# Gates of 32 more tokens placed by indirect transfers into a second table, with an order of norms at the seams of the feed-forward blocks

## The chip, the cores and the metric

The kernel runs on one core of one Trainium2 chip, alone. The metric is the device time of one execution in microseconds; runs are compared by their medians. On this core TensorE (PE) does the matrix products, VectorE (DVE) and ScalarE (ACT) the elementwise work, POOL (GpSimd) a little elementwise work and the transfers that it issues itself, and SP only issues transfers.

## What is computed

Two blocks run one after the other on 256 tokens of width 1024, in float32. The first has a gated recurrent branch and an attention branch, and after them a mixture over 16384 experts, which is the part that matters here. The second has four SwiGLU feed-forward blocks, a convolution block and a blockwise attention, each with a norm before and after it. Cut to the expert layer and the feed-forward:

```python
t1, i1 = lax.top_k(s1, 16); t2, i2 = lax.top_k(s2, 16)      # per token and head, of 128 keys each
cand = t1[..., :, None] + t2[..., None, :]                  # 16 x 16 candidates
ts, sel = lax.top_k(cand, 16)
idx = (i1 * 128 + i2) at sel
g = softmax(ts)
act = gelu(einsum('chkd,cd->chk', u[idx], xt))
out = einsum('chk,chkd->cd', g * act, v[idx])               # 8 heads x 16 experts per token

f = (silu(h @ w_gate) * (h @ w_up)) @ w_down                # feed-forward, 256 x 1024 -> 2816 -> 1024
x = x + 0.5 * rms_norm(f, g_post)
```

## The kernel before

The expert layer gathers nothing. It multiplies all 256 tokens with all 16384 rows of `peer_u`, takes the gelu, multiplies every value by the token's gate for that expert (zero for most), and multiplies the result with all of `peer_v`. The tile `C` (128 x 128 x 256) holds it: partition j and plane a stand for the expert with the two indices a and j, and the last axis is the token. Every float32 matrix operand is split into a high and a low part (`units`, L115, for weights: ScalarE writes the high half of a `ws` tile at L147, VectorE the low half at L150), and a product is three matmuls (`mm3`, L195 to L199).

The gates reach `C` in two ways. Tokens 0 to 127 are routed one head at a time (`routing_by_head`, L868). Each head gives 16 experts and 16 gates for each of 128 tokens, and POOL adds them to a table `gd` in DRAM (cleared before) with 16 indirect transfers, each of one element from each of 128 partitions (L914). Tokens 128 to 255 are routed together (`routing`, L792). Their gates are placed by `scatter` (L920), four tokens a call: VectorE and ScalarE build one-hot tiles `oh`, TensorE multiplies them (L934, four matmuls of 128 x 128), and the product goes into `C` as the factor of the gelu that is there or will come. The generator `work` (L944) hands this out in pieces between the loads of the gating stage: `peer_u` comes in 64 loads, and after each of them `advance` emits pieces up to a budget. There are 32 calls of `scatter`.

The table is cleared early: while the weights of the first projections are loaded, `clear` (L327), called at each load, adds one transfer of zeros to SP's queue, 16 of 512 KB in all.

In the expert-value stage `peer_v` comes in 64 loads, two for each group of four planes. For each of the 32 groups `gates_of` (L1030) issues from POOL a load of that group's gates of tokens 0 to 127 into one of two `x` tiles, two groups ahead; `gated_c` (L1035) multiplies four planes of `C` by it on VectorE, and `coef` (L1044) splits the group into the high and low parts that TensorE takes as the stationary side (`vgo`, L1022).

A feed-forward block (`ffn`, L1112) walks over 11 slices of its width. At its end the two halves of the tokens are taken apart: for token half 0 the post norm (`post`, L1079) and the next block's norm `nx(0)` (L1108, with `norm_only`, L246, which writes `xn` in two halves on VectorE at L253) are emitted, then the last gate and up products of half 1 (`GU`, L1119, whose result `hh` VectorE writes at L1130), then its transposes (`TR`, L1138), down products and, between them, the transposes of half 0's `xn` (`run(p0)`). I call this place a seam; there are three with a following norm that is transposed there (after blocks 0, 1 and 2).

The order on each engine is made by the Tile scheduler from the order of the program and the dependences; `after` (L162) adds an order between two instructions without a semaphore. The few lines to keep in mind:

```python
for k in range(16):                                           # routing_by_head, 16 transfers a head
    i = nc.gpsimd.indirect_dma_start(gflat, ...slot[:, h, k:k + 1]..., gate[:, h, k:k + 1], None, compute_op=ALU.add)
for k in range(32):                                           # work
    scatter(T - 4 - 4 * k, work.bound)
for t in range(2):                                            # vgo per unit of peer_v
    mm3(acc[t][half], (c[:, 0, ai % 4, ts_], c[:, 1, ai % 4, ts_]), (pair[0][:, s], pair[1][:, s]), ...)
```

## Time and profile before

| | |
|---|---|
| median of 3 runs | 2111.91 us (2111.25 to 2112.9) |
| the profiled execution, time | 2111.61 us |
| its span | 2109.8 us |
| PE busy | 2058.6 us (98%) |
| DVE busy | 1414.7 us (67%) |
| ACT busy | 1156.8 us (55%) |
| POOL busy | 347.7 us (16%) |
| DMA | 386.66 MB, mean 183 GB/s |

The span is that of the instructions in the trace; the 1.8 us beside it lie outside. Busy time is the sum of the durations of an engine's instructions, overlaps counted once. A matmul's end is modelled and successive matmuls overlap, so what one costs is read from start to start. The stages, in us from the span's start: projections, recurrent branch and attention to about 286, gating with `peer_u` to about 736, expert values with `peer_v` to about 1087, and then the second block.

### The profile page before, as it was taken

Reading aid. Unit: us, or ns where it says so; the run is one execution under the profiler, and the core shown is the slowest. Engines: PE = TensorE matmul, PEld = TensorE weight load, DVE = VectorE, ACT = ScalarE, POOL = GpSimd, SP = SyncE. Lnnn points to the kernel's source line nnn. Section 1 sums busy time; section 2 is a strip of 40 time slices with the busy share of each in tenths; the row PEclk is TensorE's granted clock in tenths of the full one; section 3 lists DMA queues with packets and bytes.
Section 4 is the critical chain, followed back from the end, with each engine's and each line's share of the span. In section 5 each row is a group of like instructions: output and inputs, shape, how many; then the busy total and the mean of one; then the engine's idle time right before and its main releaser. Section 6 shows DMA issues by size and latency. Waiting matters only on the chain.

```text
span 2109.8 us, 31786 instructions
## 1 busy us (share of the span) xinstructions
PE 2058.6 (98%) x12526; PEld 1825.8 (87%) x12526; DVE 1414.7 (67%) x2523; ACT 1156.8 (55%) x1872; POOL 347.7 (16%) x262
## 2 busy tenths in 40 slices
PE   7999999999999999999999999989999999999998
PEld 7899989999999988888878888878887888887886
DVE  6675668898877566566566665966666665756564
ACT  5885444555776444444455555565554554655553
POOL 2000007777750000000000001920000000000000
PEclk9999999999999999999999999999999999999999
DMA  8742546676654566665666554226555554744551
GB/s 269 256 141 92 178 165 164 194 184 181 179 141 146 196 213 210 215 214 206 218 246 246 182 197 142 100 72 240 196 180 173 206 182 157 263 167 180 180 196 64
DMA packets 91797, 386.66 MB, mean 183 GB/s; under 512 B 25968, under 2 KB 28144, under 8 KB 59904
## 3 DMA queue, kind: packets, MB, share of 16 engines
q1 hardware_dynamic: 70656, 376.17, 51.5%
q0 software_dynamic: 20992, 8.46, 3.1%
q8 instruction: 98, 1.61, 0.3%
q14 instruction: 51, 0.42, 0.1%
HBM read 372.87 MB, written 10.55 MB: 182 GB/s over the span
## 4 chain that ended last, share of the span: by engine, by line
PE 86%; DVE 6%; ACT 3%; DMA 2%; issue 2%; POOL 1%; SPq 0%; POOLq 0%; DVEq 0%; ACTq 0%
PE pa L197 19%; PE pa L199 19%; PE pa L198 19%; PE pt L184 6%; PE pm L184 6%; PE pt L186 3%; PE pm L186 3%; PE pm L197 2%; PE pm L199 2%; PE pm L198 2%; DVE pa L1310 2%; DVE ws L150 1%; PE pm L934 1%; ACT ws L147 1%; PE pt L234 1%
## 5 line engine op out<-in xcount | busy, mean ns | idle before, releaser
L150 DVE TENSOR_TENSOR ws<-raw,ws 128x1024 fp32r<-128x1024 f32 (+1 forms) x661 | 807.4, 1228 | 486.8 <-ACT ws L147 484.7
L147 ACT ACTIVATE ws<-raw 128x1024 fp32r<-128x1024 f32 (+1 forms) x665 | 697.4, 1056 | 577.5 <-PE pa L199 367.3
L197 PE MATMUL pa<-xT,ws 128*128 128x256 f32 x1280 | 363.6, 285 | 0.7 <-ACT g L1596 0.5
L198 PE MATMUL pa<-xT,ws 128*128 128x256 f32 x1280 | 361.4, 283 | 0.0
L199 PE MATMUL pa<-xT,ws 128*128 128x256 f32 x1280 | 361.1, 282 | 0.0
L197 PEld LDWEIGHTS pa<-xT,ws 128*128 128x128 f32 x1280 | 242.1, 189 | 1.8 <-ACT g L1596 1.0
L198 PEld LDWEIGHTS pa<-xT,ws 128*128 128x128 f32 x1280 | 242.2, 189 | 0.1
L199 PEld LDWEIGHTS pa<-xT,ws 128*128 128x128 f32 x1280 | 242.0, 189 | 0.1
L914 POOL DMA_INDIRECT gd<-gate,slot x128 | 225.4, 1761 | 99.0 <-DVE slot L909 39.1
L220 POOL TENSOR_TENSOR rr<-rs,mhalf 128x1 f32<-128x1 f32 (+1 forms) x36 | 32.3, 897 | 1203.1 <-DVE rs L218 1199.0
L198 PE MATMUL pa<-ws,ch 128*128 128x512 f32 x512 | 201.9, 395 | 0.0
L199 PE MATMUL pa<-ws,ch 128*128 128x512 f32 x512 | 201.8, 395 | 0.0
L197 PE MATMUL pa<-ws,ch 128*128 128x512 f32 x512 | 201.2, 395 | 0.0
L184 PE MATMUL pt<-xT,ws 128*128 128x512 f32 x512 | 190.6, 394 | 0.0
L184 PE MATMUL pm<-xT,ws 128*128 128x512 f32 x512 | 190.4, 394 | 0.0
L197 PE MATMUL pa<-ws,hT 128*128 128x512 f32 x352 | 139.9, 397 | 0.6 <-ACT hT L202 0.5
L199 PE MATMUL pa<-ws,hT 128*128 128x512 f32 x352 | 139.1, 395 | 0.3 <-DVE hT L203 0.3
L198 PE MATMUL pa<-ws,hT 128*128 128x512 f32 x352 | 139.0, 395 | 0.0
L186 PE MATMUL pm<-xT,ws 128*128 128x256 f32 x448 | 125.6, 280 | 0.0
L186 PE MATMUL pt<-xT,ws 128*128 128x256 f32 x448 | 125.6, 280 | 0.0
L197 PEld LDWEIGHTS pa<-ws,ch 128*128 128x128 f32 x512 | 96.5, 188 | 22.6
L198 PEld LDWEIGHTS pa<-ws,ch 128*128 128x128 f32 x512 | 96.5, 188 | 22.6 <-DVE ws L150 0.3
(454 smaller groups left out, 3868.0 us busy)
## 6 DMA issues: line engine op xcount, KB each, us to landing
raw<-in_ffn_dram SPq DMA_DIRECT2D x132, 1024.0 KB, 4.9
raw<-in_peer_u_dram SPq DMA_DIRECT2D x64, 1024.0 KB, 5.0
raw<-in_peer_v_dram SPq DMA_DIRECT2D x64, 1024.0 KB, 4.8
raw<-in_win_dram SPq DMA_DIRECT2D x16, 1024.0 KB, 4.9
gain<-in_gains_dram SPq DMA_DIRECT2D x17, 512.0 KB, 5.2
gd<-zero SPq DMA_DIRECT2D x16, 512.0 KB, 7.9
raw<-in_wpq_dram SPq DMA_DIRECT2D x8, 1024.0 KB, 5.1
x<-gd POOLq DMA_DIRECT2D x32, 256.0 KB, 4.7
```

The source lines that it names most:

```text
L147: i = nc.scalar.activation(hi, r, AF.Copy)
L150: self.last = (eng or nc.vector).tensor_tensor(out=lo, in0=r, in1=hi.bitcast(F32), op=ALU.subtract)
L184: nc.tensor.matmul(o, wp[0], v, start=first, stop=last)
L186: nc.tensor.matmul(o[:, 0:256], wp[1], v[:, 0:256], start=False, stop=False)
L197: nc.tensor.matmul(o, wh, xh, start=first, stop=False)
L198: nc.tensor.matmul(o, wh, xl, start=False, stop=False)
L199: nc.tensor.matmul(o, wl, xh, start=False, stop=last)
L220: nc.gpsimd.tensor_tensor(out=r2[:rows], in0=r[:rows], in1=mhalf[:rows], op=ALU.pow)
L234: nc.tensor.transpose(p[:, j * rows:(j + 1) * rows], src[:rows, (b + j) * 128:(b + j + 1) * 128], ident[:rows, :rows])
L914: i = nc.gpsimd.indirect_dma_start(gflat, bass.IndirectOffsetOnAxis(ap=slot[:, h, k:k + 1], axis=0), gate[:, h, k:k + 1], None, compute_op ...
L934: nc.tensor.matmul(p[:, k * 128:(k + 1) * 128], oh[:, k, 0:128], oh[:, k, 128:256], start=True, stop=True)
L1310: nc.vector.scalar_tensor_tensor(out=o, in0=u, scalar=w, in1=acc, op0=ALU.mult, op1=ALU.add)
```

## The change

Four things are done.

1. Tokens 128 to 159 leave `scatter`: it is called 24 times instead of 32. Their gates go into a second table `gd4` in DRAM by 32 indirect transfers (`by_quarters`): the 8 heads of a token are taken as four quarters of two heads, the indices and gates of 32 tokens x 128 are brought into a tile of 4 x 32 partitions by eight small transfers from POOL, and each of the 32 transfers places one element for each of 128 (quarter, token) pairs. In the table each quarter has its own 32 columns of a plane's 128.
2. `gates_of` loads from both tables, so POOL issues two loads of 256 KB a group instead of one. `gated_c` gets three POOL operations more, which add the four quarters together (64 columns, then 32, of four planes) and multiply `C` of tokens 128 to 159 by the sum. The second table is cleared by eight more transfers of zeros, of 1 MB each.
3. Each indirect transfer waits for the completion of all 16 of the group before its own (`wait_for`), and the first two groups' loads of the tables wait for all transfers of the last two groups.
4. At the seams of `ffn` the norm `nx(0)` is emitted behind `GU((1,), f)`, and its two `xn` instructions are ordered behind `GU.last`, the last `hh`.

```diff
+    gd4 = dp.tile([128, 128 * 128], F32, name="gd4")
...
+    def wait_for(i, js):
+        for j in js:
+            tc.add_manual_dep(i.ins, j.ins.name, mybir.DependencyInfo(mybir.DependencyClass.Sync, mybir.DependencyReason.DATA), reason="same elements")
...
-            nc.vector.scalar_tensor_tensor(out=xn[:rows, s], in0=src[:, s], scalar=r[:rows], in1=g[:rows, s], op0=ALU.mult, op1=ALU.mult)
+            i = nc.vector.scalar_tensor_tensor(out=xn[:rows, s], in0=src[:, s], scalar=r[:rows], in1=g[:rows, s], op0=ALU.mult, op1=ALU.mult)
+            if behind is not None:
+                after(i, behind)
...
-            if 0 <= i < ZN:
+            if 0 <= i < 3 * ZN // 2:
                 w = 128 * 128 // ZN
+                dst, i, w = (gd, i, w) if i < ZN else (gd4, i - ZN, 2 * w)
...
+                wait_for(i, placed[-16 - k:-k or None])
+                placed.append(i)
...
+        def by_quarters():
+            V = nc.vector
+            s0 = sl[:, 0].rearrange("p h k -> p (h k)")
+            V.tensor_scalar(s0, sli[:, 1], 128.0 * 128, tokf, ALU.mult, ALU.add)
+            V.scalar_tensor_tensor(out=s0, in0=sli[:, 0], scalar=128.0, in1=s0, op0=ALU.mult, op1=ALU.add)
+            V.tensor_tensor(out=sli[:, 0], in0=s0, in1=quarter, op=ALU.add)
+            for q in range(4):
+                s = slice(32 * q, 32 * q + 32)
+                nc.gpsimd.dma_start(slq[s], sli[0:32, 0, s])
+                nc.gpsimd.dma_start(gaq[s], sl[0:32, 2].rearrange("p h k -> p (h k)")[:, s])
+            for j in range(32):
+                i = nc.gpsimd.indirect_dma_start(qflat, bass.IndirectOffsetOnAxis(ap=slq[:, j:j + 1], axis=0), gaq[:, j:j + 1], None,
+                                                 compute_op=ALU.add)
+                wait_for(i, placed[-16 - j % 16:-(j % 16) or None])
+                placed.append(i)
...
-            for k in range(32):
+            by_quarters()
+            yield 8, 0.8
+            for k in range(24):
...
-            v = x_tile()[:, 0:512].rearrange("p (a t) -> p a t", a=4)
-            nc.gpsimd.dma_start(v, gd[:, 512 * g:512 * (g + 1)].rearrange("p (a t) -> p a t", a=4))
+            v = x_tile().rearrange("p (k a t) -> p k a t", k=2, a=4)
+            for i, table in enumerate((gd, gd4)):
+                i = nc.gpsimd.dma_start(v[:, i], table[:, 512 * g:512 * (g + 1)].rearrange("p (a t) -> p a t", a=4))
+                if g < 2:
+                    wait_for(i, placed[-32:])
...
-            G(nc.vector.tensor_tensor(out=c, in0=c, in1=gl.pop(0), op=ALU.mult))
+            v = gl.pop(0)
+            G(nc.vector.tensor_tensor(out=c, in0=c, in1=v[:, 0], op=ALU.mult))
+            w, c = v[:, 1], C[:, 4 * g:4 * g + 4, 128:160]
+            nc.gpsimd.tensor_tensor(out=w[:, :, 0:64], in0=w[:, :, 0:64], in1=w[:, :, 64:128], op=ALU.add)
+            nc.gpsimd.tensor_tensor(out=w[:, :, 0:32], in0=w[:, :, 0:32], in1=w[:, :, 32:64], op=ALU.add)
+            nc.gpsimd.tensor_tensor(out=c, in0=c, in1=w[:, :, 0:32], op=ALU.mult)
...
-            p0 = nx(0)
             GU((1,), f)
+            p0 = nx(0, GU.last)
```

The order that the scheduler makes of it, at the places of which the prediction speaks. First VectorE at the seam after the first feed-forward block, before the change (`hh` is the product of gate and up half, `xn` the normed tokens, `ws` a weight's low half, `hT` the low half of the transposed `hh`):

```order
L150 TENSOR_TENSOR ws<-raw,ws 128x1024
L253 SCALAR_TENSOR_TENSOR xn<-x,rr,gain 128x512 x2
L1130 TENSOR_TENSOR hh<-pm,sg 128x256
L150 TENSOR_TENSOR ws<-raw,ws 128x1024
L203 TENSOR_TENSOR hT_12333<-pt,hT_12332 128x2x128
```

And with the change:

```order
L152 TENSOR_TENSOR ws<-raw,ws 128x1024
L1177 TENSOR_TENSOR hh<-pm,sg 128x256
L259 SCALAR_TENSOR_TENSOR xn<-x,rr,gain 128x512 x2
L209 TENSOR_TENSOR hT_12397<-pt,hT_12396 128x2x128
L152 TENSOR_TENSOR ws<-raw,ws 128x1024
```

`hh` now stands ahead of `xn`, right behind the same `ws`, and `hT` ahead of the next `ws`. At the third seam one `ws` stays between `xn` and `hT`; elsewhere the three are alike. TensorE's order there is all but the same in both, and what is to be noted in it is that the transposes of `xn` come right behind those of `hh`:

```order
L240 MATMUL pt<-ident,hh 128x128 x2
L240 MATMUL pt<-ident,xn 128x128 x4
L203 MATMUL pa<-ws,hT_12396 128x512
L204 MATMUL pa<-ws,hT_12396 128x512
L203 MATMUL pa<-ws,hT_12396 128x512
L205 MATMUL pa<-ws,hT_12397 128x512
```

Last POOL's queue with the change, from the heads' transfers to the steady state of the expert-value stage (`gd_67` is the second table):

```order
L924 DMA gd<-gate,slot 2097152x1 x64
L969 DMA gaq<-sl 32x32 x4
L924 DMA gd<-gate,slot 2097152x1 x32
L968 DMA slq<-sli 32x32 x4
L924 DMA gd<-gate,slot 2097152x1 x32
L971 DMA gd_67<-gaq,slq 2097152x1 x32
L1072 DMA x<-gd 128x512
L1072 DMA x<-gd_67 128x512
...
L1082 TENSOR_TENSOR x<-x 128x4x64
L1083 TENSOR_TENSOR x<-x 128x4x32
L1084 TENSOR_TENSOR C<-C,x 128x4x32
```

Before, the heads' 128 transfers are followed directly by the 32 gate loads, with nothing between them. From the fifth group on, the last five of these rows repeat for each group, and the first of the three operations waits for the load just ahead of it.

## Rows read from the trace of the kernel before

**Rows 1.** The page, part 4: the chain that ended last, by engine.

```profile
PE 86%; DVE 6%; ACT 3%; DMA 2%; issue 2%; POOL 1%; SPq 0%; POOLq 0%; DVEq 0%; ACTq 0%
```

**Rows 2.** Two stages: PE, PEld, DVE, ACT, POOL busy us, clock, DMA share, GB/s.

```profile
555.00:690.00 135.00, 135.00 (x1156) 135.00 (x1155) 101.97 (x185) 93.69 (x231) 47.87 (x30) 1.00 0.52 152
...
735.00:1075.00 340.00, 340.00 (x1476) 276.05 (x1476) 203.26 (x186) 160.62 (x157) 15.31 (x28) 1.00 0.61 211
```

**Rows 3.** Who TensorE waited for, whole span: us in total, times, longest.

```profile
PE pt L234 <- DVE hh L1130: 5.7, 3, 2.0
```

**Rows 4.** TensorE's timeline round one pair of scatter steps: start, us, instruction.

```profile
671.32 0.28 PE L199 MATMUL pa<-xT,ws 128*128 128x256 f32 x1
671.44 1.95 PE L934 MATMUL pm<-x 128*128 128x128 f32 x16
673.14 0.36 PE L197 MATMUL pa<-xT,ws 128*128 128x256 f32 x1
673.35 0.27 PE L198 MATMUL pa<-xT,ws 128*128 128x256 f32 x1
```

**Rows 5.** VectorE's timeline at the end of the first feed-forward block.

```profile
1282.34 1.22 DVE L150 TENSOR_TENSOR ws<-raw,ws 128x1024 fp32r<-128x1024 f32 x1
1284.00 1.41 DVE L253 SCALAR_TENSOR_TENSOR xn<-x,rr,gain 128x512 f32<-128x512 f32 x2 [0.44 <-POOL rr L220]
1285.33 0.42 DVE L1130 TENSOR_TENSOR hh<-pm,sg 128x256 f32<-128x256 f32 x1
```

**Rows 6.** TensorE's timeline at the same place.

```profile
1285.80 0.44 PE L234 MATMUL pt<-ident,hh 128*128 128x128 f32 x2 [1.98 <-DVE hh L1130]
1286.07 0.60 PE L234 MATMUL pt<-ident,xn 128*128 128x128 f32 x4
1286.71 0.55 PE L197 MATMUL pa<-ws,hT 128*128 128x512 f32 x1
```

**Rows 7.** The stretches behind the first two seams, columns as in rows 2.

```profile
1285.00:1300.00 15.00, 13.64 (x87) 12.18 (x88) 11.12 (x18) 8.98 (x15) 1.48 (x2) 0.89 0.60 209
...
1605.00:1625.00 20.00, 18.89 (x90) 15.18 (x91) 14.94 (x24) 9.89 (x19) 1.95 (x2) 1.00 0.68 239
```

**Rows 8.** Transfers issued from 24 to 45 us: KB each, median us to landing.

```profile
raw<-in_win_dram SPq DMA_DIRECT2D x3, 1024.0 KB, 7.3
```

**Rows 9.** SP's timeline: the third weight load of the projection stage.

```profile
110.97 0.33 SPq L131 DMA_DIRECT2D raw<-in_win_dram  x1
```

**Rows 10.** ScalarE's timeline: the first use of that load.

```profile
117.90 1.05 ACT L147 ACTIVATE ws<-raw 128x1024 fp32r<-128x1024 f32 x1
```

**Rows 11.** POOL's timeline: second head's first transfer, the last transfer, two gate loads.

```profile
357.29 1.54 POOL L914 DMA_INDIRECT gd<-gate,slot  x1 [4.00 <-DVE wk L800]
...
612.73 1.54 POOL L914 DMA_INDIRECT gd<-gate,slot  x1 [0.30 <-issue]
...
888.97 0.55 POOL L1032 DMA_DIRECT2D x<-gd  x1 [10.62 <-DVE C L1037]
...
900.13 0.55 POOL L1032 DMA_DIRECT2D x<-gd  x1 [10.61 <-DVE C L1037]
```

**Rows 12.** POOL by line and form: busy us, mean ns of one, idle before.

```profile
L914 POOL DMA_INDIRECT gd<-gate,slot x128 | 225.4, 1761 | 99.0 <-DVE slot L909 39.1 <-issue 37.1 <-DVE ws L150 6.8
...
L150 POOL TENSOR_TENSOR ws<-raw,ws 128x1024 fp32r<-128x1024 f32 x4 | 9.4, 2374 | 5.5 <-ACT ws L147 5.5
...
L1329 POOL TENSOR_TENSOR pw<-pw 128x256 f32<-128x256 f32 x1 | 1.6, 1588 | 0.1
```

**Rows 13.** VectorE's timeline where the expert-value stage begins.

```profile
731.55 1.29 DVE L1037 TENSOR_TENSOR C<-C,x 128x512 f32<-128x512 f32 x2
```

**Rows 14.** Transfers issued from 735 to 850 us, columns as in rows 8.

```profile
x<-gd POOLq DMA_DIRECT2D x10, 256.0 KB, 4.7
```

**Rows 15.** VectorE's timeline in the convolution.

```profile
1317.08 4.05 DVE L150 TENSOR_TENSOR ws<-raw,ws 128x1024 fp32r<-128x1024 f32 x2
```

**Rows 16.** POOL's timeline at the same time.

```profile
1317.24 2.81 POOL L1326 TENSOR_TENSOR pw<-ud,pv 128x1024 f32<-128x1024 f32 x1 [16.77 <-DVE ud L1346]
```

More of the change, by code (lines that the diff above doesn't have):

```diff
@@ L244, in norm_T, with norm_only @@
         norm_only(src, g, wk, rows, r, (hi, lo, off))()
-    def norm_only(src, g, wk, rows, r, dst):
+    def norm_only(src, g, wk, rows, r, dst, behind=None):
         hi, lo, off = dst
@@ L328, in clear @@
             i -= ZFROM
-            if 0 <= i < ZN:
+            if 0 <= i < 3 * ZN // 2:
                 w = 128 * 128 // ZN
-                nc.sync.dma_start(gd[:, i * w:(i + 1) * w].rearrange("p (r w) -> p r w", w=512),
+                dst, i, w = (gd, i, w) if i < ZN else (gd4, i - ZN, 2 * w)
+                nc.sync.dma_start(dst[:, i * w:(i + 1) * w].rearrange("p (r w) -> p r w", w=512),
                                   zero.unsqueeze(1).to_broadcast([128, w // 512, 512]))
@@ L755, in _body @@
         st.aside = None
-        assert st.calls >= ZFROM + ZN
+        assert st.calls >= ZFROM + 3 * ZN // 2
         dump("h1", X[0])
@@ L863, in _body @@
         posu1 = cp.tile([128, 16], U32, name="posu1")
+        placed = []
         gflat = gd.rearrange("p (e o) -> (p e) o", o=1)
@@ L939, in scatter @@
                 nc.scalar.activation(C[:, bound:128, t0:t0 + 4], v[:, bound:128, :], AF.Copy)
+        quarter = cp.tile([128, 128], I32, name="quarter")
+        nc.gpsimd.iota(quarter, [[32, 4], [0, 32]], base=0, channel_multiplier=0)
+        slq = cp.tile([128, 32], I32, name="slq")
+        gaq = cp.tile([128, 32], F32, name="gaq")
+        qflat = gd4.rearrange("p (e o) -> (p e) o", o=1)
+        def by_quarters():
[13 more added lines that the diff above has]
+                placed.append(i)
+                tc.declare_no_dep(i.ins, group="quads%d" % (j // 16), reason="other elements")
+                tc.add_to_no_dep_group("quads%d" % (j // 16), i.ins)
         class Scattered:
@@ L1015, in _body @@
             advance(WQBUD * 8 + BUD * (n + 1) if n < 62 else 1e9)
-        assert Scattered.done == 128
+        assert Scattered.done == 96
         dump("idT", idT)
@@ L1106, in __init__, with __call__ @@
                 self.xT = [joined(alloc) for _, alloc in items]
-            def __call__(self, t):
+            def __call__(self, t, behind=None):
                 r = rstd([X[t]], D, bp)
-                return [norm_only(X[t], g, bp, 128, r, (x[0], x[1], t * 128)) for g, x in zip(self.g, self.xT)]
+                return [norm_only(X[t], g, bp, 128, r, (x[0], x[1], t * 128), behind) for g, x in zip(self.g, self.xT)]
         def ffn(i, xT, nxt, pend):
@@ L1129, in GU @@
                     nc.scalar.activation(sg, p[t][:, 0:256], AF.Silu)
-                    nc.vector.tensor_tensor(out=h, in0=p[t][:, 256:512], in1=sg, op=ALU.mult)
+                    GU.last = nc.vector.tensor_tensor(out=h, in0=p[t][:, 256:512], in1=sg, op=ALU.mult)
                     hh[t, f] = h
@@ L1634, in _body, with __call__ @@
             xT = None
-            def __call__(self, t):
+            def __call__(self, t, behind=None):
                 for half in range(2):
```

## The prediction

> **What bounds the kernel now.** I read the chain of waits first: 86% of it is TensorE, and no other engine has over 6% [rows 1]. So time is won by taking instructions from TensorE or by shortening its waits, and work put on another engine is free until TensorE waits for it. Next the stages. While the gating stage places gates and multiplies with `peer_u`, TensorE is busy in all of its 135 us, VectorE in 102, ScalarE in 94. In the expert-value stage TensorE is busy in all of 340 us, VectorE in 203, and POOL in 15 [rows 2]. In both stages only TensorE's own instructions set the time. Last the list of TensorE's waits. Most are single and lie at borders of stages; one repeats, for `hh` at the seams: 5.7 us in three waits [rows 3]. The change takes TensorE work out of the first stage, shortens these three waits, and puts work on POOL and on the DMA queues, where the room is.
>
> **Eight scatter steps fewer.** A pair of steps is one stretch of matmuls [rows 4]. Ordinary matmuls there start 0.12 us apart (671.32 to 671.44). Without the pair the two behind it would start at 671.44 and 671.56; the second starts at 673.35. A pair costs 1.79 us, a step 0.895 us, eight steps 7.15 us. Nothing else fills TensorE's time in this stage, so all of it comes off. VectorE's and ScalarE's share of the eight steps lay beside TensorE's work and gives nothing.
>
> **The seams.** Today `xn` waits for its norm's factor until 1284.00, and `hh`, whose inputs are there, stands behind both halves of `xn` until 1285.33 [rows 5]. TensorE's transposes of `hh` start at 1285.80 after 1.98 us of waiting, so its last matmul had ended at 1283.82 [rows 6]. With the change `hh` follows the `ws` that ends at 1283.56 and is done 0.42 us later, at 1283.98; the transposes start at about 1284.0. But the next thing in TensorE's queue is the transposes of `xn`, and `xn` is no earlier than now: it starts at 1284.00, and its first half is done after half of the 1.41 us that the two take, plus a little of the pipeline, at about 1284.75. So `xn`'s transposes start at 1284.8, and by the distance in today's rows the down matmuls 0.64 us behind them, at 1285.44 instead of 1286.71. The saving is 1.27 us and not 1.98: what is late next is `xn`. The low half of the transposed `hh` now follows `xn` at 1285.41 and takes as long as `hh`, 0.42 us; it is done by 1285.85, before the fourth matmul needs it. At the third seam a `ws` of 1.22 us stands between, and I take 0.3 us off there. Three seams: 3.5 us. The bounds are 5.7 us (the whole wait) and nothing (if TensorE stands as long for `xn`); I stay near the worked value, since each of its terms is a row. Beside it the granted clock is 0.89 in the 15 us behind the first seam, and 1.00 in the 20 us behind the second [rows 7], after nearly equal waits; a shorter wait may keep the clock up there, which would give up to 15 x 0.11 = 1.7 us more. I don't count it.
>
> **Zeros for the second table.** Eight transfers of 1 MB go into SP's queue between the weight loads at 95 to 160 us, in front of which TensorE must not run dry. Beside the zeros of today a weight load takes 7.3 us to land [rows 8]. The third of the loads in question is issued at 110.97 and first used by ScalarE at 117.90 [rows 9, 10], so there are 6.9 us. By these rows a load would be 0.4 us late; eight of them make 3.2 us if nothing hides it. Three `ws` tiles lie between ScalarE and TensorE and hide most. I take 0.5 us, near the lower end, with bounds of 0 and 3.2. The few reordered instructions of this stage go in with that.
>
> **POOL's longer queue.** The 128 transfers end at 612.73 + 1.54 = 614.3 us today [rows 11]. They already stand for about 4 us at a head's start; the row names VectorE there, but heads were computed long before, and what they wait for is the transfer in front. The full waits are then mostly met: I count nothing for them within the eight heads. Added are eight small transfers of at most 0.85 us each (0.55 to issue and 0.30 between): up to 6.8 us; a gap of 4.0; two groups of 16 at 1.76 + 0.30 us [rows 12], 65.9 us; a gap of 4.0 between them, and 4.0 to land: the tables are complete at 699 at the latest. Four gate loads (3.4 us) land 4.7 us later [rows 14], and three operations of POOL take about 2 us (below): 709. VectorE multiplies the first group at 731.55 today [rows 13], which becomes 724.4. There are 15 us to spare, so this costs nothing; from then on every microsecond POOL is late would be a microsecond lost.
>
> **POOL in the expert-value stage.** A group lasts 11.16 us (888.97 to 900.13) [rows 11]. POOL's cycle is: wait for VectorE's multiply, issue two loads (2 x 0.85), wait for the second to land (4.7), add and multiply. The three operations have 256, 128 and 128 elements a partition. Scaling the 2.37 us for 1024 gives 0.6 + 0.3 + 0.3 = 1.2 us; the single row of 256 elements has 1.59 us, three of these 4.8 [rows 12]. I take 2.0, nearer the scaling, since it stands on four instructions. The cycle is 8.4 us, below 11.16, and the result is needed a group later still. It costs nothing.
>
> **VectorE beside POOL.** Where POOL began an operation beside VectorE's weight subtractions, two of these took 4.05 us together, against 1.22 for one [rows 15, 5], while POOL's lasted 2.81 [rows 16]. So the two engines do hold each other up, here by about 1.6 us. In the expert-value stage VectorE is busy in 203 of 340 us [rows 2], 6.7 of 11.16 a group, and has 4.5 to spare; 2 us of holding up go into that. I count nothing. The Trainium skill's page "SBUF — State Buffer", section "Who interferes with whom", says that a VectorE instruction with two SBUF inputs contends with a GpSimd instruction that reads SBUF and that the loser blocks fully for the instruction's whole length; the row agrees, and by the rule all three of POOL's new operations in a group could stand against VectorE, which makes the last rival below.
>
> **The sum.** -7.15 (scatter) -3.5 (seams) +0.5 (zeros) = -10.15 us. The profiled execution took 2111.61 us, its span and 1.8 us around it, and gives 2101.5. The median of the runs, 2111.91, is 0.3 us above that execution; I state the time against it: 2101.8 us.
>
> **The rivals.**
>
> 1. The seams' wait only moves to `xn`. For it: the transposes of `xn` stand right behind those of `hh`, and `xn` starts no earlier. Against it: half of `xn` suffices. Then 2111.9 - 7.15 + 0.5 = 2105.3.
> 2. The seams give their whole 5.7 us and the clock 1.7 us: 2111.9 - 7.15 - 5.7 - 1.7 = 2097.4. Against it: the worked order has `xn` late.
> 3. The zeros cost their 3.2 us: 2111.9 - 7.15 - 3.5 + 3.2 = 2104.5. Against it: the same mixture of loads and zeros earlier in this stage leaves no long wait.
> 4. The change does not do what it says on TensorE: its queue is shorter but waits for weights, as loads and their splits now come no sooner. For it: nothing but that VectorE's 102 of 135 us is high. The scatter term is then lost by two thirds: 2111.9 - 2.4 - 3.5 + 0.5 = 2106.5 at best and about 2109 if the seams fail too.
> 5. Slower: POOL's cycle becomes the bound of the expert-value stage. It decides when the cycle passes 11.16 us. With three operations of 1.59 us and a load that lands as late as a weight beside zeros, 7.3 us [rows 8], it is 1.7 + 7.3 + 4.8 = 13.8. At half a microsecond over, 11.66, thirty groups lose 15 us: 2101.8 + 15 = 2117; at 13.8 far more. For it: the second load doubles what a group fetches. Against it: only the two worst rows together get there.
> 6. POOL's operations take 4.8 us a group and all stand against VectorE: 6.7 + 4.8 = 11.5 against 11.16, 0.3 us in each of 32 groups, 10 us: 2112, no change.
>
> **How the numbers follow.** Forecast 0.61, rival 1 0.10, rival 2 0.08, rival 3 0.08, rival 4 0.06, rival 5 0.05, rival 6 0.02. A measurement of this kernel tells about 0.2%, 4.2 us, from no change. Forecast and rivals 1 to 3 are faster by more than that, 0.87; rivals 4 and 6 lie within it, 0.08; rival 5 is slower, 0.05. The range reaches from rival 2 to rival 4's better case, 2097.4 to 2106.5, and leaves out half of rival 4 and rivals 5 and 6, about 0.1, and as much for what I have not seen.
>
> **What would show it.** Right: the L934 group has 192 records in place of 256, and the stage to the first `peer_v` matmul is 7 us shorter; TensorE's wait for `hh` at the seams falls from 5.7 us to under 1, and a new one for `xn` of about half a microsecond stands behind each; POOL's last transfer starts before 700, and in the expert-value stage TensorE still shows no idle time, with the same 11.16 us a group. Wrong: groups longer than 11.16 with ScalarE's split of `C` waiting for POOL (rival 5) or for VectorE (rival 6), a wait of TensorE behind 724, or waits for weights in the projections.

## The result, and the profile after

The changed kernel takes **2096.61 us** (median of 4 runs, 2095.41 to 2097.1), the kernel before 2111.74 (2111.25 to 2112.9): 15.1 us less, a ratio of 0.9927 with a 95% interval of 0.9910 to 0.9944. Forecast were 2101.8 us and a range of 2097.4 to 2106.5. The sign was right, the gain was 15 us and not 10, and the time lies 0.8 us below the range. Of the six executions of the seams alone, further below, one took 2895.02 us at a granted clock of 0.655 over its span and is left out of the ratio there.

The profiled execution took 2096.59 us with a span of 2094.8, against 2111.61 and 2109.8. To see where the 15.0 us went, each TensorE instruction of one trace was paired with the same one of the other, and the difference of their starts was followed through the program:

| place (us in the kernel before) | this place alone | forecast |
|---|---|---|
| start to 555 | +0.6 | +0.5 |
| gating stage, 555 to 736 | -7.1 | -7.15 |
| expert-value stage, 736 to 1087 | 0.0 | 0 |
| first seam, 1284 to 1292 | -3.1 | -1.3 |
| between first and second seam | -0.2 | 0 |
| second seam, 1604 to 1607 | -1.4 | -1.3 |
| one wait for `hT` at 1638 | -0.6 | 0 |
| third seam, 1794 to 1798 | -0.9 | -1.0 |
| 15 us behind the third seam | -1.6 | 0 |
| last matmul to the end of the span | -0.7 | 0 |

The first three rows came out as worked. The surplus lies at the first seam (the three together gave 5.4 against 3.5) and in the last rows, which the sum did not have.

The chain that ended last, as shares of the span by engine, against [rows 1]:

```profile
PE 87%; DVE 6%; ACT 3%; issue 2%; POOL 1%; DMA 1%; SPq 0%; DVEq 0%; POOLq 0%; ACTq 0%
```

Who TensorE waited for (us in total, times, longest) no longer has a row for `hh` [rows 3]. `xn` has three waits more than before, each of 0.51 us (first before, then after):

```profile
PE pt L234 <- DVE xn L253: 12.4, 5, 7.3
...
PE pt L240 <- DVE xn L259: 13.9, 8, 7.7
```

TensorE's timeline at the first seam, where [rows 6] had a wait of 1.98 us (start, duration, instruction, idle time before it):

```profile
1277.39 0.44 PE L240 MATMUL pt<-ident,hh 128*128 128x128 f32 x2
1278.34 0.63 PE L240 MATMUL pt<-ident,xn 128*128 128x128 f32 x4 [0.51 <-DVE xn L259]
1278.72 0.48 PE L203 MATMUL pa<-ws,hT 128*128 128x512 f32 x1
1279.04 0.40 PE L204 MATMUL pa<-ws,hT 128*128 128x512 f32 x1
1279.27 0.40 PE L203 MATMUL pa<-ws,hT 128*128 128x512 f32 x1
```

VectorE's at the same place, against [rows 5]:

```profile
1275.79 1.22 DVE L152 TENSOR_TENSOR ws<-raw,ws 128x1024 fp32r<-128x1024 f32 x1
1276.92 0.41 DVE L1177 TENSOR_TENSOR hh<-pm,sg 128x256 f32<-128x256 f32 x1
1277.44 1.41 DVE L259 SCALAR_TENSOR_TENSOR xn<-x,rr,gain 128x512 f32<-128x512 f32 x2
```

`hh` starts where the `ws` ends, its transposes follow without a wait, and half a microsecond is spent on `xn`, as the prediction had it. The last two matmuls show what it did not have: they start 0.23 us apart. In the kernel before, the matmuls behind the same seam started 0.43 us apart, for 3.5 us:

```profile
1287.06 0.63 PE L198 MATMUL pa<-ws,hT 128*128 128x512 f32 x1
1287.48 0.63 PE L197 MATMUL pa<-ws,hT 128*128 128x512 f32 x1
```

The stretch of 15 us around the seam (busy time of PE, PEld, DVE, ACT and POOL, granted clock, DMA share, GB/s), and the expert-value stage, against [rows 7] and [rows 2]:

```profile
1275.80:1290.80 15.00, 13.73 (x96) 12.15 (x95) 13.24 (x22) 10.56 (x17) 3.38 (x3) 1.00 0.71 215
...
729.60:1080.00 350.40, 350.40 (x1516) 283.99 (x1515) 232.17 (x191) 166.78 (x168) 138.73 (x146) 1.00 0.68 239
```

The granted clock is 1.00 behind the first seam instead of 0.89. In the expert-value stage TensorE is still busy all the time. The scatter's group of TensorE (busy us, mean ns of one) has 192 records, eight for each of 24 steps; a pair of steps in [rows 4] has 16:

```profile
L946 PE MATMUL pm<-x 128*128 128x128 f32 x192 | 23.5, 275 | 0.0
```

POOL's timeline: the last transfer, the first gate loads, and one group of the expert-value stage, against [rows 11]:

```profile
683.09 1.54 POOL L971 DMA_INDIRECT gd<-gaq,slq  x1 [0.30 <-issue]
686.81 2.28 POOL L1072 DMA_DIRECT2D x<-gd  x4 [2.18 <-ACT C L1052]
...
861.55 1.12 POOL L1072 DMA_DIRECT2D x<-gd  x2 [1.98 <-DVE C L1080]
867.06 1.64 POOL L1082 TENSOR_TENSOR x<-x 128x256 f32<-128x256 f32 x1 [4.38 <-DMA x<-gd]
868.77 1.33 POOL L1083 TENSOR_TENSOR x<-x 128x128 f32<-128x128 f32 x1
870.18 1.33 POOL L1084 TENSOR_TENSOR C<-C,x 128x128 f32<-128x128 f32 x1
872.36 1.12 POOL L1072 DMA_DIRECT2D x<-gd  x2 [0.85 <-DVE C L1080]
```

The last transfer starts at 683.1, and the gate loads that wait for it at 686.8, earlier than the 699 worked out as the latest. A group of POOL is issue, landing, three operations and a wait for VectorE's multiply, which is 0.9 to 2.0 us here: the only slack left in it, as it seems.

Last the place 15 us behind the third seam. VectorE, before:

```profile
1804.52 0.14 DVE L218 TENSOR_SCALAR rs<-rs 128x1 f32<-128x1 f32 x1
1804.58 1.22 DVE L150 TENSOR_TENSOR ws<-raw,ws 128x1024 fp32r<-128x1024 f32 x1
1806.23 1.41 DVE L1090 SCALAR_TENSOR_TENSOR x<-y,rr,x 128x512 f32<-128x512 f32 x2 [0.44 <-POOL rr L220]
```

and after:

```profile
1791.28 0.14 DVE L224 TENSOR_SCALAR rs<-rs 128x1 f32<-128x1 f32 x1
1791.44 0.69 DVE L209 TENSOR_TENSOR xT<-pt,xT 128x512 fp32r<-128x512 f32 x1
1792.15 1.42 DVE L1137 SCALAR_TENSOR_TENSOR x<-y,rr,x 128x512 f32<-128x512 f32 x2
```

From the end of `rs` to `x` it was 1.57 us and is now 0.73, because a weight piece that stood between them is now behind `x`, and the short `xT` that stood ahead of `rs` covers POOL's part of the norm. The norm of the second half of the tokens is on TensorE's path here: TensorE's wait for its `xn`, before and after, was

```profile
1812.45 1.29 PE L234 MATMUL pt<-ident,xn 128*128 128x128 f32 x8 [0.86 <-DVE xn L253]
...
1798.37 0.63 PE L240 MATMUL pt<-ident,xn 128*128 128x128 f32 x4 [0.53 <-DVE xn L259]
```

and two further waits behind it, of 0.16 and 0.47 us, are gone. No line of the change names this place: the scheduler placed the weight piece anew once `hh` and `xn` had changed places.

The last row of the table is a wait of POOL's sequencer at the end of the program. The instructions of its last line, before and after (duration in ns: shortest, median, longest; first and last start):

```profile
L1719 POOLq DRAIN  x3: 46/102/5080, 2104.0 to 2109.6; - x3
...
L1766 POOLq DRAIN  x3: 46/102/3855, 2089.7 to 2094.5; - x3
```

The longest of them took 5.08 us and was the last thing waited for; with the change it takes 3.85 and ends before SP's own wait for the last stores. So it is in all traces: 5.08 in the seven without the second table, 3.85 in the six with it. Why it is shorter is open.

### The profile page after: what moved, and what is told of

Same layout as the page of the kernel before. It is cut to its first block, busy times and chain, and to the rows that moved or that the text cites. A ratio compares the mean times of both kernels' runs of the same rounds, so it can differ in the third digit from the quotient of the medians.

```text
span 2094.8 us, 31832 instructions
## 1 busy us (share of the span) xinstructions
PE 2048.3 (98%) x12462; PEld 1816.3 (87%) x12462; DVE 1424.6 (68%) x2494; ACT 1145.9 (55%) x1832; POOL 534.1 (25%) x431
## 4 chain that ended last, share of the span: by engine, by line
PE 87%; DVE 6%; ACT 3%; issue 2%; POOL 1%; DMA 1%; SPq 0%; DVEq 0%; POOLq 0%; ACTq 0%
PE pa L203 19%; PE pa L205 19%; PE pa L204 19%; PE pt L186 6%; PE pm L186 6%; PE pt L188 3%; PE pm L188 3%; PE pm L203 2%; PE pm L205 2%; PE pm L204 2%; DVE pa L1357 2%; DVE ws L152 2%; PE pm L946 1%; PE pt L240 1%; POOL rr L226 1%
## 5 line engine op out<-in xcount | busy, mean ns | idle before, releaser
L152 DVE TENSOR_TENSOR ws<-raw,ws 128x1024 fp32r<-128x1024 f32 (+1 forms) x661 | 819.5, 1247 | 469.2 <-ACT ws L149 466.9
```

The source lines that it names most:

```text
L152: self.last = (eng or nc.vector).tensor_tensor(out=lo, in0=r, in1=hi.bitcast(F32), op=ALU.subtract)
```

## The experiments

The runs below were made in three groups, each beside runs of the kernel before. These spread more than in the first measurement (2106.0 to 2114.8 in 23 runs of the first group, median 2110.31; medians 2112.15 and 2114.08 in the other two), so differences of 1 to 3 us are read from the paired starts of TensorE's instructions, as above, and the times only say whether they fit.

### Seams alone

On the kernel before, the part of the change on `norm_only`, `Pre`, `NoPre` and `GU.last`, and

```
             post(0, pd[0], gpost, 0.5)
-            p0 = nx(0)
             GU((1,), f)
+            p0 = nx(0, GU.last)
```

> The kernel before with the order at the seams alone: hh ahead of xn on VectorE in all ffn blocks; 32 scatter steps, one table. Theory A (the seams are worth about 7 us by themselves: first seam 3.0, of which 1.6 is the clock that no longer falls behind the wait, second 1.5, third 0.8, and 1.5 more some 15 us behind the third, where VectorE takes a weight piece behind a norm instead of ahead of it): 2111.7 - 6.8 = 2104.9, with 2104.0 to 2105.8; matmuls behind the first seam start 0.23 us apart instead of 0.43. Theory B (the seams are worth the 3.5 us forecast, and the rest of the surplus comes with the earlier start of the late stages that the scatter's saving brings): 2108.2, with 2107.7 to 2108.7.

Measured: 2103.14 us (before 2110.31; ratio 0.9961, 0.9948 to 0.9974). By the paired starts: first seam -3.0, second -1.4, third -0.9, behind the third -1.65, 1638 us -0.6, and -0.5 between the first two seams; -8.1 in all. Theory A, rather more than it asked for (the time lies 0.9 us below its range, beside a kernel before that is 1.4 us faster in this group); theory B is out. The surplus belongs to the seams' part of the change, not to the scatter.

### All but the seams

On the changed kernel, the three lines of the seam put back.

> The changed kernel with xn ahead of hh again at the seams; second table, 24 scatter steps and full waits stay. Theory A: 2111.7 - 7.1 (scatter) + 0.6 (early stage) = 2105.2, with 2104.7 to 2105.8; the wait for hh is back at 5.7 us in three, and the matmuls behind the first seam start 0.43 us apart. Theory B: 2096.6 + 3.5 = 2100.1, with 2099.6 to 2100.8, and the clock behind the first seam stays up although the wait is back.

Measured: 2103.8 us (ratio 0.9964, 0.9950 to 0.9977). Gating -7.1, seams 0.0 at all three, behind the third -0.3; the early stage +1.15. TensorE's timeline at the first seam, and the 15 us from there (columns as above):

```profile
1279.85 0.44 PE L240 MATMUL pt<-ident,hh 128*128 128x128 f32 x2 [1.91 <-DVE hh L1177]
```

```profile
1279.05:1294.05 15.00, 13.68 (x87) 12.24 (x88) 11.13 (x18) 9.02 (x15) 1.51 (x2) 0.89 0.58 210
```

With the wait of 1.9 us the lower clock behind it is back as well. Theory A by the starts; the time lies 0.9 us below its range, for the reason given above, and well above theory B's.

### The third seam alone

On the kernel before, the order of `nx` and `GU` changed in the third feed-forward block only:

```
+            if i not in (2,):
+                p0 = nx(0)
             GU((1,), f)
+            if i in (2,):
+                p0 = nx(0, GU.last)
```

> The kernel before with hh ahead of xn at the third seam alone (the ffn block ahead of the key and value projections). Theory A: 0.8 us at the seam and 1.5 us where the weight piece moves behind the norm, 2111.7 - 2.3 = 2109.4, with 2108.9 to 2109.9; nothing changes at the first two seams. Theory B: 1.0 us at the seam alone, 2110.7, with 2110.4 to 2111.2, and TensorE's wait for xn 15 us behind it stays at 0.86 us.

Measured: 2109.03 us (ratio 0.9991, 0.9982 to 1.0), in the range of theory A, which says little beside a kernel before at 2110.31. By the starts it is -0.8 at the seam and -1.7 behind it, as theory A has it. But something at the first seam, where nothing had been changed, fits neither theory. The wait, and the 15 us from there:

```profile
1286.73 0.44 PE L234 MATMUL pt<-ident,hh 128*128 128x128 f32 x2 [1.97 <-DVE hh L1132]
```

```profile
1285.93:1300.93 15.00, 13.48 (x98) 12.45 (x99) 12.01 (x20) 9.80 (x16) 1.94 (x2) 1.00 0.64 224
```

The same wait of 1.97 us was followed by the full clock, and the stretch gained 1.5 us. So a wait of this length may lower the clock or not.

### TensorE kept busy in the first wait

On the kernel before:

```
             DN(1, f - 1)
+            if i == 0:
+                idle = ps("pt")
+                for k in range(8):
+                    nc.tensor.matmul(idle, hT[f - 1][0][:, 1, 128:256], dnw[f - 1][1][0][:, 0:512], start=True, stop=True)
             TR(1, f)
```

> The kernel before with eight further matmuls of 128x512 on TensorE in its wait for hh at the first seam; their results go to a bank that nobody reads. The wait itself stays (hh is no earlier), only TensorE is busy in it. Theory A (1.6 us of the first seam's gain is the clock): the matmuls behind the wait start 0.23 us apart instead of 0.43, the granted clock in the 15 us behind is above 0.95 instead of 0.89, and the time is 2111.7 - 1.6 = 2110.1, with 2109.6 to 2110.6. Theory B (the slow stretch has another cause than the idle time, or the work behind waits for something else): no gain, 2111.4 to 2112.2.

Measured: 2110.92 us against 2110.31 (ratio 0.9998, 0.9988 to 1.0008): no gain in time, and in neither theory's range. TensorE's timeline:

```profile
1283.95 1.98 PE L1216 MATMUL pt<-ws,hT 128*128 128x512 f32 x8
1286.09 0.44 PE L234 MATMUL pt<-ident,hh 128*128 128x128 f32 x2 [0.17 <-DVE hh L1130]
...
1287.34 0.39 PE L198 MATMUL pa<-ws,hT 128*128 128x512 f32 x1
1287.57 0.39 PE L197 MATMUL pa<-ws,hT 128*128 128x512 f32 x1
```

At its place the expectation of theory A held: `hh` is no earlier, the matmuls behind it start 0.23 us apart, and the first seam gains 1.6 us. So 1.6 us of the first seam's 3.1 are the clock and 1.5 the wait. But in this execution the clock was lower behind the second and the third seam, whose waits nobody had touched (1.86 and 1.83 us), and each lost 1.6 us; in the convolution there was one fall fewer than before, 1.7 us. What one wait gave, the others took.

### The kernel before once more

No edit.

> The kernel before, unchanged, in a further execution. Theory A (a wait of 1.8 to 2.0 us of TensorE at a seam is followed by the lower clock in some executions and not in others): the three waits for hh are as long as in the first execution, 1.8 to 2.0 us, and the seams behind which matmuls run 0.43 us apart need not be the first alone; none, two or others are as likely. Theory B (the first seam's place in the program decides): the first seam and it alone again.

Measured: one run, 2108.91 us. Waits of 1.94, 1.86 and 1.83 us; the lower clock behind the first alone, as theory B has it and as theory A allows. With the runs above and below, B does not hold for the place in general: over the executions in which `hh` came behind `xn`, 19 waits of 1.6 to 2.0 us (one of 1.62, the others of 1.83 or more) were followed by the lower clock 8 times. Six executions had the wait at the first seam: in four it fell there and nowhere else, in one (the second table alone, below) behind the second and the third, in one (the third seam alone) not at all; with the first wait filled it fell behind the other two. What decides is not shown. Two more things can be read here. The starts at 1638 us came 0.6 us earlier than in the first profile without any change, so those 0.6 us of the table belong to that one execution (0.4 of them come again in two others, the third seam alone and the second table alone). And the stages up to 555 us were 1.8 us shorter, so differences of the early stage below 2 us can't be read from starts.

### Half of each wait filled

As above, with four matmuls in place of eight, in each of the three blocks.

> The kernel before with four further matmuls of 128x512 in TensorE's wait for hh at each of the three seams, so that about 1.0 us of each wait of 1.9 is left; their results are read by nobody. Theory A (the shorter TensorE stands, the less often the clock falls behind it: never yet after 0.5 us, 7 times in 16 after 1.8 to 2.0): three waits of 0.9 to 1.1 us, and no fall behind any of them or one at most. Theory B (any wait will do, and the seams with hh first were lucky): two or three falls. The time is that of the kernel before within 2 us, as the end of each wait is set by hh.

Measured: one run, 2106.78 us. Waits of 1.07, 0.91 and 0.93 us, and no lower clock behind any: theory A. Together at the seams: 8 falls behind 19 waits of 1.6 to 2.0 us, none behind 3 of about 1.0, none behind 16 of 0.51 (five executions with all seams changed, and the third seam alone). The time missed its expectation: it is 2.1 us below the run just above and 5.3 below the lowest of the seven beside it. By the starts, against the first execution of the kernel before, 1.6 us are the first seam's clock and 3.9 lie in the convolution, where two falls are missing; 1.8 are lost in the second feed-forward block, where the clock fell behind a wait of 1.38 us.

By chance the scheduler also moved the weight piece behind the norm here, with `xn` still ahead of `hh` at all seams:

```profile
1800.73 0.15 DVE L218 TENSOR_SCALAR rs<-rs 128x1 f32<-128x1 f32 x1
1800.88 0.69 DVE L203 TENSOR_TENSOR xT<-pt,xT 128x512 fp32r<-128x512 f32 x1
1801.60 1.41 DVE L1090 SCALAR_TENSOR_TENSOR x<-y,rr,x 128x512 f32<-128x512 f32 x2
```

The starts behind it came 1.7 us earlier (from -3.2 to -4.9). So these 1.7 us are this order of VectorE's, whatever brought it about.

### The scatter alone

On the kernel before, `range(24)` in place of `range(32)`.

> The kernel before with 24 scatter steps in place of 32 and nothing else: the gates of tokens 128 to 159 are not placed at all, so that part of the result is left out. Theory A (each step is 0.895 us of TensorE's own time, and nothing of the saving is used up by the second table): 7.1 us less in the gating stage, the early stage within 0.3 us of the kernel before, 2111.7 - 7.1 = 2104.6, with 2103.8 to 2105.4. Theory B (the saving of 7.1 in the changed kernel is what is left of a larger one, because the second table's work beside it holds TensorE up): over 7.6 us, under 2104.1.

Measured: 2104.25 us (ratio 0.9959, 0.9944 to 0.9975); -7.1 in the gating stage. The early stage was 0.8 us shorter, which is outside the 0.3 us asked for and within what it varies by. Theory A: nothing of the saving is used up by the second table. At the end of the program the span was 8.01 us from the last matmul's start to its end, as in all seven executions without the second table, while the six with it had 7.25 to 7.27. These 0.7 us come with the second table; they are POOL's wait at the end of the program, shown above.

### The second table alone

The changed kernel without the seams and with all 32 scatter steps.

> The changed kernel without its seams and with all 32 scatter steps: the gates of tokens 128 to 159 are placed twice, so these tokens get them doubled; all that the second table costs is in it, and none of the gain. Theory A (it costs the early stage 0.6 us and nothing else, as POOL's longer queue ends 30 us before it is needed): 2111.7 + 0.6 = 2112.3, with 2111.3 to 2113.0; gating and expert-value stages as long as before within 0.3 us. Theory B (in the changed kernel it fitted only because TensorE had eight steps fewer): at least 2 us more in the gating stage, 2114 or more.

Measured: 2113.07 us (ratio 1.0007, 0.9998 to 1.0016). The two stages in windows, columns as in [rows 2]:

```profile
555.00:736.50 181.50, 181.50 (x1548) 181.50 (x1547) 127.17 (x212) 115.82 (x263) 111.34 (x74) 1.00 0.59 165
736.50:1087.00 350.50, 350.50 (x1507) 281.85 (x1506) 227.43 (x191) 166.50 (x168) 132.00 (x146) 1.00 0.68 238
```

TensorE stands in neither, and the first matmul with `peer_v` starts at 737.31 against 737.66: theory B is out, and the gating stage is as theory A has it. The expert-value stage is not: TensorE's starts slip by 1.4 us through it, where 0.3 was asked for. The slip is even, each matmul 0.4% further from the one ahead, at a granted clock of 1.00. The changed kernel and the run without the seams have the same work in this stage and do not slip; the run with twice the work on POOL (below) slips by the same 1.4. So the slip is not to be laid to the second table's work alone, and its cause is open. The median lies 0.1 us above theory A's range; the slip is part of that, and the lower clock came behind two seams here, the second and the third, where the first execution of the kernel before had it behind one, the first. The zeros' price is in the early stage: TensorE's wait for weights at 107 to 112 us was 2.17 to 2.19 us in all executions without the second table, and 2.4 to 3.2 in those with it.

### Twice the work on POOL

On the changed kernel, three more additions in each group:

```
             nc.gpsimd.tensor_tensor(out=w[:, :, 0:64], in0=w[:, :, 0:64], in1=w[:, :, 64:128], op=ALU.add)
+            for k in (0, 1, 2):
+                nc.gpsimd.tensor_tensor(out=w[:, :, 64:128], in0=w[:, :, 0:64], in1=w[:, :, 64:128], op=ALU.add)
```

> The changed kernel with three more additions of 256 elements a partition on POOL in each group of the expert-value stage; they write numbers that nobody reads. Theory A (POOL is near its bound: in a group of 11.2 us it stands 0.9 to 2.0 us for VectorE's multiply, and all the rest is issue, landing and operations): three more operations at 0.8 to 1.6 us bring its cycle from about 10 to 13 or 14 us, every one of some 30 groups is 2 to 3 us longer, and the time is 2096.6 + 30 x 2.5 = 2172, with 2145 to 2200. Theory B (the landing is waited for only because POOL comes early; the loads are a group ahead and the cycle closes up): POOL still fits, under 2100.

Measured: one run, 2097.04 us. Theory A fell, by 75 us. A group of POOL's timeline:

```profile
861.11 0.74 POOL L1082 TENSOR_TENSOR x<-x 128x256 f32<-128x256 f32 x1 [3.46 <-DMA x<-gd]
861.93 3.23 POOL L1084 TENSOR_TENSOR x<-x 128x256 f32<-128x256 f32 x3
865.24 1.33 POOL L1085 TENSOR_TENSOR x<-x 128x128 f32<-128x128 f32 x1
866.65 0.46 POOL L1086 TENSOR_TENSOR C<-C,x 128x128 f32<-128x128 f32 x1
867.11 1.11 POOL L1072 DMA_DIRECT2D x<-gd  x2
872.56 0.74 POOL L1082 TENSOR_TENSOR x<-x 128x256 f32<-128x256 f32 x1 [4.34 <-DMA x<-gd]
```

The slack was wider than the wait for VectorE said. The additions cost 1.1 us each (3.23 for three here), the wait for VectorE's multiply is gone, and the last operation of the group takes 0.46 us here, 0.62 on average, where it had taken 1.31. 11.45 us pass from one group to the next here (861.11 to 872.56). Over the stage TensorE's starts slip by 0.05 us a group, evenly, but so they did above with three operations, so this does not tell of POOL. What does is when ScalarE splits the group that POOL has finished at 867.11:

```profile
878.69 1.05 ACT L208 ACTIVATE ch<-C 128x1024 fp32r<-128x1024 f32 x1
```

That is 11.6 us later. From the fifth group on POOL is ahead of the split by 9.3 to 12.0 us and does not fall back; in the changed kernel it is ahead by 17 to 20. So rival 5's edge lies beyond six operations; how far is not shown.

### The other waits of the changed kernel filled

On the changed kernel, `busy(n, tag)` issues n transposes of `ident` into one bank, behind the last matmul, with n = 36 ahead of `finish(1)`, 16 ahead of the first block's first `GU`, 22 ahead of the convolution's projection 6, 32 ahead of `silu_c(0)`.

> The changed kernel with further transposes of the unit matrix on TensorE, whose results nobody reads, in the four waits behind which its matmuls still run at the lower clock: 36 ahead of the second norm's transposes (3.5 us), 16 ahead of the first gate matmul of the first ffn block (1.6 us), 22 in the convolution's wait for ud (2.1 us), 32 ahead of the transposes of rows (3.1 us). Theory A (what costs time behind a wait is that the clock falls, and work in the wait keeps it up): 1.4 + 1.8 + 1.7 + 1.3 = 6.2 us less, 2096.6 - 6.2 = 2090.4, with 2089.4 to 2093.0 and no stretch of matmuls of 512 columns 0.43 us apart behind these waits. Theory B (the clock falls for another reason, or falls at the next wait instead): 2095.5 to 2098.

Measured: 2094.37 us (2093.36 to 2095.97): 2.2 us of the 6.2, and in the profiled execution even these lie in the first 265 us, where nothing was changed. The time lies between the two theories' ranges. The first filling gave 1.2 us. The second gave none: the clock stayed up, but the matmuls then stood for `ws` (0.35 and 0.96 us), which had been hidden under the lower clock. The third stood behind the projection whose wait it should fill and cost 2.4 us of its own (behind the wait itself, which was not filled, the clock stayed up this time, 1.5 us). The fourth held TensorE 1.0 us longer than its wait had, and behind the next long wait the clock fell instead, for 1.6 us (TensorE's timeline of the second feed-forward block):

```profile
1407.33 0.50 PE L211 MATMUL pm<-ws,xT 128*128 128x512 f32 x1 [1.38 <-DVE xT L215]
...
1408.30 0.63 PE L211 MATMUL pm<-ws,xT 128*128 128x512 f32 x1
1408.72 0.63 PE L209 MATMUL pm<-ws,xT 128*128 128x512 f32 x1
```

### The fillings at their places

The same with 31, 18 (ahead of projection 4), 24 (into another bank), and 10 ahead of the second block's first `GU`; none at the first block.

> The changed kernel with further transposes of the unit matrix, read by nobody, in four waits, each now as long as the wait and at its place: 31 ahead of the second norm's transposes, 18 in the convolution's wait for ud, between the matmuls on either side of it, 24 ahead of the transposes of rows, 10 ahead of the second ffn block's first gate matmul; none at the first ffn block, where the next weight piece sets the pace. Theory A (each fall that is avoided gives back what it cost: 1.4 + 1.7 + 0.9, and the fall that moved to the second ffn block stays away too): 2096.6 - 4.0 = 2092.6, with 2091.5 to 2094.0. Theory B (a fall avoided at one wait comes at another, or the added work stands in the way): 2094.5 to 2097.

Measured: **2091.05 us** (2089.65 to 2091.68) against 2114.08 for the kernel before beside it: ratio 0.9886, 0.9870 to 0.9903, where the changed kernel had 0.9927. That is 0.45 us below theory A's range. Against the changed kernel's trace, the first filling gave 1.3 us, the second 1.5 and the two others 1.5 together. The stretches behind the first and the third filling (columns as above), in the changed kernel

```profile
280.00:300.00 20.00, 16.43 (x100) 14.64 (x99) 11.52 (x19) 8.01 (x12) 0.89 (x3) 0.91 0.31 100
...
1374.00:1394.00 20.00, 16.17 (x83) 13.55 (x82) 9.71 (x24) 12.41 (x30) 5.25 (x4) 0.83 0.15 52
```

and here

```profile
280.00:300.00 20.00, 19.64 (x144) 17.82 (x143) 11.37 (x18) 8.41 (x12) 0.89 (x3) 1.00 0.40 137
...
1370.00:1390.00 20.00, 18.17 (x116) 15.62 (x115) 10.38 (x24) 13.03 (x30) 5.90 (x4) 1.00 0.17 57
```

show the granted clock up from 0.91 and 0.83 to 1.00. Over all executions, the lower clock came behind the first of these waits (3.5 us) in 11 of 11 that left it open and in neither of the two that filled it, behind the third (2.3 to 3.1) in 10 of 11 and in neither. Behind the second (2.1) it came in 8 of 12 that left it open, so the one execution that filled it does not show that the filling kept the clock up. This version beats both kernels: its interval lies below the changed kernel's.

## Why the prediction was right and wrong

**Eight scatter steps: right.** -7.15 forecast, -7.1 in the changed kernel, in the kernel without the seams, and with the scatter alone. A pair's price, read from one pair [rows 4], held for four of them.

**The zeros: right.** +0.5 forecast. By the starts it was +0.6, which alone would prove nothing, as the early stage varies; by TensorE's wait for weights there it is 0.2 to 1.0 us over six executions. The cause was the one named.

**POOL's longer queue: right.** Ready before 699 forecast; the last transfer starts at 683.1 and the loads behind it at 686.8. The stage behind it lost nothing.

**POOL in the expert-value stage: right in result, sizes loose.** The operations took 0.96, 1.31 and 1.31 us on average, 3.6 together where 2.0 was taken and 4.8 was the bound. Rival 5 was further off than the trace of the change alone suggests: six operations in place of three still fitted.

**VectorE beside POOL: right that it costs nothing.** In the expert-value stage VectorE went from 203 us in 340 [rows 2] to 232 in 350.4: the kernel before has 209.8 in the same stretch, so it is 22 us in 32 groups, 0.7 us a group where 2 was allowed and 4.5 were spare. POOL's three operations last 3.6 us a group. The Trainium skill's page "SBUF — State Buffer", section "Who interferes with whom", says that a VectorE instruction with two SBUF inputs contends with a GpSimd instruction that reads SBUF, and that the lock on the shared port pair is exclusive; by that, rival 6's 4.8 us a group were possible. The rows agree with the rule as far as both engines' instructions grow longer where they meet (POOL's additions of 1.3 us all stood beside busy VectorE, VectorE's weight subtractions went from 1.23 to 1.32 us on average), but the price on VectorE is a fifth of POOL's busy time, not the whole of it. Part of that busy time is what VectorE costs POOL: the shortest rows of the three operations, in the run with POOL's work doubled, are 0.74, 0.46 and 0.46 us, 1.7 together.

**The seams: the step that failed.** "Three seams: 3.5 us." The waits themselves gave 1.5, 1.4 and 0.9, 3.8 together, so the mechanism and its size were right, `xn` late by 0.51 us included. Two things were missing in the term.

The first is the clock at the first seam. The prediction saw it [rows 7], priced it at up to 1.7 us, and wrote "I don't count it". It is 1.6 us: the run with the filled wait gives it without the wait, the run without the seams loses it. Beside it stands only that the second seam kept the full clock after a nearly equal wait, and that is no reason to put it at nothing. That one of three equal waits was followed by the lower clock says that such a wait is followed by it sometimes, and with three of them about one fall was to be expected in any execution: 8 in 19 in the runs here. The change removes the waits and so the falls; that gain belonged in the sum, at 8 in 19 times 1.6 us for each of three seams, 2.0 us. That the profiled execution of the kernel before had exactly one was luck; others had none or two. Rival 2 was the right rival for the clock and had 0.08.

The second, which the prediction did not see, is the 1.6 us behind the third seam. The prediction looked at the seams and at the early stage for what the scheduler had moved, and not at the next norm behind a seam. The comparison of the two orders of VectorE's instructions shows the weight piece moved there, and the timeline of the kernel before shows the 0.44 us for POOL's part and the 1.22 us of `ws` ahead of a norm for which TensorE then stands 0.86 us. By these rows it could have been seen, and priced at up to the 0.86 us of that wait. Of the 1.6 us, 1.0 are waits of TensorE (three of 1.5 us together became one of 0.53); where the rest lies was not traced.

With these two the seams' term is 3.8 + 1.6 + 1.6 = 7.0 us, and the sum 2101.8 - 3.5 = 2098.3. The rest down to 2096.6 is 0.7 at the program's end, which no row of the prediction showed, 0.6 that the first profile of the kernel before had lost at 1638 us by itself, and 0.4 of small ones.

**The range.** Its lower end was rival 2, the whole wait and the clock; the sum of that rival leaves out the zeros' 0.5 us, with which it is 2097.9. Both bounds of the seams' term were taken within the seams' own rows; an effect behind them lay outside any bound.

## What to carry to other kernels

When a wait of TensorE is removed, price three things: the wait, the lower clock behind it in those executions where it falls, and what the scheduler moves further on; a fall seen behind one of three equal waits is a chance to be counted for all three. Where a wait must stay, useless matmuls or transposes of the wait's length keep the clock up; by one execution of each filling, they pay only where the matmuls behind are not about to wait for weights, where they stand in the wait and not ahead of or behind it, and where the next long wait is filled as well. An engine's idle time in one place of its loop is not its slack: doubling its work for one run tells whether it fits, though not where the edge is.

## What was not expected of the hardware

- Waits of TensorE of 1.6 to 2.0 us at the seams were followed by its lower clock (1.2 GHz, matmuls of 512 columns 0.43 us apart instead of 0.23) in 8 of 19 cases, with the same program behind them; waits of 0.9 to 1.1 us in none of 3 and of 0.51 us in none of 16. Each fall there cost 1.5 to 1.6 us. Elsewhere in the thirteen executions, where the wait was left open, the matmuls behind a wait of 1.4 us ran at the lower clock in 2 of 12, behind 2.1 in 8 of 12, behind 2.3 to 3.1 in 10 of 11 and behind 3.5 in 11 of 11. Ahead of the first feed-forward block, waits of 0.2, 0.4 and 0.8 us stand within 3 us, and the matmuls behind them ran at the lower clock in 10 of 12; so the length of one wait does not tell it all.
- Transposes of a 128x128 unit matrix in float32, 0.11 us each, kept the clock up through waits of 3.1 and 3.5 us in the two executions that had them there; eight matmuls did through one of 1.97 us.
- A POOL operation of 128 elements a partition took 0.46 us at best and mostly 1.3 to 1.5 in the loop of the changed kernel (59 of 60 were over 0.7 us); with POOL's work doubled, 40 of 60 took 0.46. The long ones of the expert-value stage all stood beside VectorE at work.
- The program's end, from the last matmul's start, was 0.7 us shorter in every execution with the second table (7.25 to 7.27 against 8.01 us): POOL's last drain took 3.85 us and not 5.08. Why it did stays open.
- In two executions of thirteen all matmuls of the expert-value stage stood 0.4% further apart, 1.4 us in 350, at a granted clock of 1.00 and without a wait. Why stays open.
